# A decayed cumulative sum behind a matmul: new engine orders for the first 40 tiles, and a fourth input buffer

## The chip, the cores and the metric

The kernel runs on one core of a Trainium2 chip. Five engines work side by side, each through its own queue in order: TensorE (PE, the matmuls), VectorE (DVE), ScalarE (ACT), GpSimd (POOL) and SyncE (SP, which here only issues DMAs). The metric is the device time of one execution in microseconds (us); lower is better.

## What is computed

```python
x, w, decay = inputs            # (16, 2048, 1024), (1024, 1024), (1024,), all float32
xw = x @ w                      # per batch: 2048 time steps, 1024 output channels
out[:, 0, :] = xw[:, 0, :]
for t in range(1, S):           # S = 2048
    out[:, t, :] = decay[None, :] * out[:, t - 1, :] + xw[:, t, :]
```

It is a matmul, followed by a running sum over time that shrinks by a factor of its own in every channel.

## The kernel before

**Chunks and tiles.** The time axis of a batch is cut into four chunks of 512 steps, so there are 64 chunks. Two neighbouring chunks make a group. A tile (the code says slot) is one group times one of eight blocks of 128 output channels: 1024 time steps in PSUM, 128 channels on the partitions, and 16 matmuls of 128x512 (eight contraction blocks k, two chunks). Tiles 0 to 7 belong to chunks 0 and 1, tiles 8 to 15 to chunks 2 and 3, and so on. Chunks 0 and 1 hold the first half of a batch, chunks 2 and 3 the second, so tiles 8 to 15 continue the sums of tiles 0 to 7 from saved last columns (keep).

**Input path.** A chunk comes in four loads (L105), each 256 KB in bf16, cast by the DMA and issued from GpSimd's queue into a buffer xb (three of them). VectorE turns it (turn, L115, letter T: 32x32 blocks of two-bf16 words) into xw, and ScalarE sorts it into xt in two parts (part, L123): X for contraction blocks 0 to 3, Y for 4 to 7. At the start chunks 0 and 1 go in smaller pieces: E turns a quarter chunk (half of the time steps, half of the channels), and F (VectorE) or G (ScalarE) copies an eighth. M loads half a chunk.

**Weights.** w comes in eight pieces into the room of output buffers; settle (L299) casts or copies one contraction block for four channel blocks into wsb, as W on VectorE or as w on ScalarE. Pieces 0 to 7 serve tiles 0 to 3, pieces 8 to 15 tiles 4 to 7 (and all later ones): 8 to 11 the even k, 12 to 15 the odd k. U loads such a piece's data. D makes the decay columns and their squares.

**Scans.** An unpaired tile is scanned by VectorE straight from PSUM, 1024 elements long (S, L216). A paired tile is done at half that length: ScalarE copies PSUM to xs (p, L178) and makes decay times the even steps (g, L164), GpSimd adds that to the odd steps (j, L191), VectorE scans the 512 odd steps with the squared decay (S, L196), ScalarE multiplies the result by the decay (h, L164) and GpSimd adds it to the even steps (c, L241). P stands for p, g, z and j together, C for h and c (and k, which saves the last column; z puts the starting value in front of the result). Whether a tile is paired is its place among four (three are, the fourth is not), turned around for the tiles in `flips`. The squares lie in SBUF until deed d (L342) puts a second copy into PSUM, which later scans use.

**Output.** VectorE turns the result back (B, L253) into an output buffer; when four tiles are in it, SyncE issues four stores.

**PSUM.** Tiles use three buffers of 1024 columns in turn, so tile s+3 can begin when tile s has left its buffer: by S for an unpaired tile, by p and g for a paired one. Tile 3 lies in two spare buffers; tiles 4, 5 and 6 follow tiles 0, 1 and 2.

**Order.** Everything is issued in program order, and an engine does its queue strictly in that order. The program goes through the tiles; behind the matmuls of each it performs a list of deeds (L547 to L556), each a letter and a number: S5 is the scan of tile 5, T4 the turn of chunk 4, L the next load in `loads`. Which deeds stand behind which tile is written out by hand in `agenda` for the prologue (-99), the first 17 and the last 20 tiles; between them usual() makes the list, with the turns and copies of chunks at set distances ahead (`later`). A deed's place against other engines' deeds does not matter, only its place in its own engine's queue.

```python
        self.paired = n % R != R - 1
        if len(tiles) in flips or len(tiles) - len(slots) in flips:
            self.paired = not self.paired
```

Of the kernel before, what the change touches and what calls it, by code (L numbers as in the profile page):

```python
# [25 lines left out]
def kernel(  # L26
# [31 lines left out]
    NQ = 4  # L58
# [17 lines left out]
    def ring(pool, name, count, shape, dtype=FP32):  # L76
        i = turns[name] = turns.get(name, -1) + 1
        return pool.tile(shape, dtype, name=f"{name}{i % count}")
# [22 lines left out]
    def load(c, q, j0=0, j1=NJ):  # L101
        b, t0 = chunks[c]
        if c not in xb_of:
            xb_of[c] = ring(sb, "xb", 3, [128, NJ, CQ], BF16)
        pin(nc.gpsimd.dma_start(  # L105
            out=xb_of[c][quad(q), j0:j1],
            in_=_ap(x, [[D, P], [P * D, j1 - j0], [1, CQ]],
                    (b * S + t0 + j0 * P) * D + q * CQ)))
# [246 lines left out]
    def ending(i):  # L355
        b, t0 = chunks[-1]
        nb = TL // 128
        pts = [ring(psp, name, count, [128, R, 128])
               for name, count in (("spare1", 1), ("ps", 3), ("ps", 3), ("spare", 1))]
        wides = [ring(sb, *spot, [128, NQ, R, P])  # L360
                 for spot in (("xb", 3), ("xb", 3), ("xb", 3), ("h", 4))]

        def cross(blocks, rs):
            for i in blocks:
                for r in rs:
                    t = 2 + i * 128
                    pin(nc.tensor.transpose(  # L367
                        out=pts[i][:, r], in_=tiles[r - R].so[:, t:t + 128], identity=ident))

        def leave(i, copy):  # L370
            pin(copy(out=wides[i].rearrange("p q r i -> p r q i"),
                     in_=pts[i].rearrange("p r (q i) -> p r q i", q=NQ)))
            pin(nc.sync.dma_start(
                out=_ap(out, [[D, 128], [1, CH]], (b * S + t0 + i * 128) * D + CH),
                in_=wides[i].rearrange("p q r i -> p (q r i)")))

        cross((0,), range(R))
        cross((1,), range(R))
        cross((2, 3), range(R - 1))
        cross((2, 3), (R - 1,))  # L380
        for i in range(nb):
            leave(i, (nc.scalar.copy, nc.vector.tensor_copy)[i % 2])
# [2 lines left out]
    slots += [([c], n) for c in groups[-1] for n in range(K)]  # L385
    tiles = []

    def turn_and_load(c):
        turn(c)
        if 2 <= c < nch - 3:  # L390
            loads.extend((c + 3, q) for q in range(NQ))

    loads = [(c, q) for c in (2, 3, 4) for q in range(NQ)]
    deeds = {
        "P": lambda s: tiles[s % len(slots)].pair(),
        "S": lambda s: tiles[s % len(slots)].scan(),
        "C": lambda s: tiles[s % len(slots)].complete(),
        "B": lambda s: tiles[s % len(slots)].back(),
        "T": turn_and_load,
        "X": lambda c: part(c, nc.scalar.copy, 0, 2),  # L400
        "Y": lambda c: part(c, nc.scalar.copy, 2, M),
        "x": lambda c: part(c, nc.vector.tensor_copy, 0, 2),
# [21 lines left out]
        "L": lambda i: load(*loads.pop(0)) if loads else None,  # L424
    }
    agenda = {
        -99: "M0 M1 U0 U1 M2 M3 U2 U3 W0 w1 L E0 F0 G1 E1 L F2 D G3 E2 F4 L G5 W2 E3 F6 w3 G7 W4 W6 w5 w7 E4 F8 G9 E5 F10 G11 E6 F12 G13 E7 F14 G15 W8 W10 W9 W11",
        0: "P0 L w15 w13",
        1: "L L L S0 C0",
        2: "L P2 P1 w12 S1 L L B0 B1 S2",  # L430
        3: "w14 C2 T2",
        4: "S3 P4 X2 Y2 T3 C1",
        5: "",
        6: "L L P5 L B3 L L S4 L S5 B2 C3 X3 Y3 C4 T4",
        7: "P6 C5 S7 X4 S6",
        8: "C7 C6 L d P8 B4 B7 B6",
        9: "B5 P9",
        10: "L S8 P10 C8 T5 X5 L S9",
        11: "L L S11 L C9 Y4 S10 C10 B8",
        12: "",  # L440
        13: "B11 P12 B10 B9 Y5 S12 P13 C12",
        14: "L P14 T6 S13 C13 L Y6 L",
        15: "L S15 L S14 C14",
        16: "B13 B12 B15 B14 P16 X6",
        -20: "z-20",
        -19: "p-20 g-20",
        -18: "j-20 S-19 S-20 k-19 B-19",
# [15 lines left out]
        -2: "S-3 S-4",  # L463
        -1: "S-2 h-4 c-4 a-1 b-1 V",
    }
    flips = (0, 1, -19, -18, -16, -11, -8, -6, -3, -2)
    later = {10: ["Y4"]}
    for c in range(5, nch):
        first = c // 2 * K
        ahead = (7, 6, 4) if c % 2 else (11, 10, 8)  # L470
        for letter, a in zip("TXY", ahead):
            later.setdefault(first - a, []).append(f"{letter}{c}")

    def usual(s):
        paired = [t.paired for t in tiles]
# [25 lines left out]
    for step, (g, n) in enumerate(slots):  # L501
        T = TL * len(g)
        left = step - len(slots)
        if n % R == 0:
            ns, nj = range(n, n + R), T // P
            outlets = [Outlet(ns, nj)]
        if left == -R:
            outlets = []
        if step == 0:
            heads = [ring(psp, "ps", 3, [128, T]) for _ in range(3)]  # L510
            firsts = [ps[:, 0:TL] for ps in heads] + [spares[0]]
            seconds = [ps[:, TL:T] for ps in heads] + [spares[1]]
            for j0, j1 in halves:
                for k in (0, 2):
                    for i in range(R):
                        matmul(firsts[i], i, k, xt_of[0], j0 * P, j1 * P)
            for k in (4, 6, 1, 3, 5, 7):
                for i in range(R):
                    matmul(firsts[i], i, k, xt_of[0])
            for k0 in range(0, K, 4):  # L520
                for i in range(R):
                    for k in range(k0, k0 + 4):
                        matmul(seconds[i], i, k, xt_of[1], 0, H * P)
            for i in range(R):
                for k in range(K):
                    matmul(seconds[i], i, k, xt_of[1], H * P, TL, H * P)
        if step < R:
            ps = heads[n] if n < 3 else tuple(spares)
        else:
            if len(g) == 2 or n % R < 3:  # L530
                ps = ring(psp, "ps", 3, [128, T])
            else:
                ps = ring(psp, "spare", 1, [128, TL])
            todo = [(k, l) for k in range(K) for l in range(len(g))]
            if step < K:
                todo.sort(key=lambda kl: kl[0] % 2)
            elif step == K:
                todo.sort(key=lambda kl: kl[1])
            if left == -1:
                ps = tuple(both[:, t:t + TL // 2] for t, both in zip(  # L540
                    (0, TL // 2), (ps, ring(psp, "ps", 3, [128, TL]))))
                for t, half in zip((0, TL // 2), ps):
                    for k in range(K):
                        matmul(half, n, k, xt_of[g[0]], t, t + TL // 2, t)
                todo = []
            for k, l in todo:
                matmul(ps[:, l * TL:(l + 1) * TL], n, k, xt_of[g[l]])  # L547
        tiles.append(Tile(g, n, ps, outlets))
        do = agenda.get(step, agenda.get(left) if left >= -20 else None)
        if do is None:  # L550
            do = usual(step)
        else:
            do = do.split()
            if left == -20:
                do = rest(step) + do
        perform(do)  # L556
# [29 lines left out]
```

## Time and profile before

| | |
|---|---|
| time, median of 5 runs | 910.46 us (910.19 to 912.15) |
| the profiled execution's own time | 909.47 us |
| its span, first to last instruction | 907.4 us |
| TensorE busy | 895.1 us, 99% of the span |
| VectorE, ScalarE, GpSimd busy | 830.0, 679.8, 655.0 us |
| first matmul on data | 10.16 us |
| tile 4, tile 9 begin | 28.48, 47.49 us |
| granted TensorE clock | 1.000 |

The span leaves out what lies around the program's instructions, here 2.1 us. Busy time of TensorE is the union of its matmuls, which overlap each other; how fast it works is better read from how many matmuls fit in a stretch. Rows of the timeline give the start and the length of an instruction, or of several alike that follow each other (xN), and in brackets the idle time of the engine before it with what ended that.

### The profile page before, as it was taken

To read this page: it belongs to the slowest core of one execution; us is meant where nothing else is said; L and a number is where in the kernel's file an instruction comes from. 1 tells how busy PE (TensorE), PEld (TensorE's weight loads), DVE (VectorE), ACT (ScalarE), POOL (GpSimd) and SP (SyncE) were. 2 spreads that over 40 slices of the span, in tenths; PEclk is the share of its full clock that TensorE was granted. 3 is DMA by queue.
4 is the path that set the end of the run, shared out by engine and by line. 5 is a ranking of instruction groups with operands and counts; after the bars stand their busy time and mean duration, and the time that the engine had idled before them with its cause. 6 is when DMAs were issued, how large, how long until landed. Compare 5 with 4: busy or idle time off the path is not lost.

```text
span 907.4 us, 12011 instructions
## 1 busy us (share of the span) xinstructions
PE 895.1 (99%) x4187; PEld 409.9 (45%) x4187; DVE 830.0 (91%) x620; ACT 679.8 (75%) x940; POOL 655.0 (72%) x754
## 2 busy tenths in 40 slices
PE   7999999999999999999999999999999999999997
PEld 3544444444444444444444444444444444444444
DVE  4999999999999999999999999999999999999998
ACT  3787887877777778778778777787787787787742
POOL 7677978777777777677687776777777776876632
PEclk9999999999999999999999999999999999999999
DMA  9999999999999999999999999999999999999868
GB/s 166 175 222 236 216 215 253 245 258 251 243 244 249 242 231 234 221 231 231 223 234 221 231 229 224 236 228 226 233 228 228 224 237 222 227 230 213 178 143 235
DMA packets 402604, 204.48 MB, mean 225 GB/s; under 512 B 8816, under 2 KB 401776, under 8 KB 402544
## 3 DMA queue, kind: packets, MB, share of 16 engines
q1 hardware_dynamic: 265200, 134.76, 59.6%
q0 software_dynamic: 137344, 68.96, 57.0%
q8 instruction: 32, 0.52, 0.2%
q14 instruction: 28, 0.23, 0.1%
HBM read 138.42 MB, written 134.22 MB: 300 GB/s over the span
## 4 chain that ended last, share of the span: by engine, by line
PE 94%; DMA 2%; ACT 1%; DVE 1%; POOL 1%; issue 0%; DVEq 0%; POOLq 0%
PE ps L126 93%; DMA xb<-in_x_dram 1%; ACT xt L123 1%; PE spare L126 1%; DMA ot<-in_w_dram 1%; DVE so L216 0%; POOL ot L291 0%; ACT h L164 0%; POOL xb L105 0%; ACT xs L178 0%; DVE ot L253 0%; DVE so L196 0%; PE spare L367 0%; DVE wsb L299 0%; PE ps L367 0%
## 5 line engine op out<-in xcount | busy, mean ns | idle before, releaser
L126 PE MATMUL ps<-xt,wsb 128*128 128x512 bf16 (+1 forms) x4086 | 877.9, 377 | 5.4 <-DVE xt L123 2.8
L126 PEld LDWEIGHTS <-wsb 128*128 128x128 bf16 x4144 | 405.2, 98 | 485.9 <-issue 5.8
L191 POOL TENSOR_TENSOR xs<-h,xs 128x512 f32<-128x512 f32 (+1 forms) x188 | 240.5, 1279 | 200.8 <-ACT h L164 96.6
L178 ACT COPY xs<-ps 128x1024 f32<-128x1024 f32 (+1 forms) x188 | 187.7, 998 | 156.8 <-PE ps L126 155.0
L253 DVE STREAM_TRANSPOSE ot<-so 128x1024 f32<-128x1024 f32 (+1 forms) x260 | 299.8, 1191 | 0.8
L241 POOL TENSOR_TENSOR so<-h,xs 128x512 f32<-128x512 f32 (+1 forms) x188 | 239.5, 1274 | 38.5 <-ACT h L164 21.7
L123 ACT COPY xt<-xw 128x2048 bf16<-128x2048 bf16 (+1 forms) x132 | 240.6, 1824 | 9.6 <-DVE xw L115 9.6
L105 POOL DMA_DIRECT2D xb<-in_x_dram x264 | 174.0, 660 | 1.6 <-POOLq L570 0.9
L164 ACT ACTIVATE h<-so,dec 128x512 f32<-128x512 f32 (+1 forms) x188 | 144.0, 766 | 30.1 <-DVE so L196 26.7
L115 DVE STREAM_TRANSPOSE xw<-xb 128x2048 f32<-128x2048 f32 (+1 forms) x70 | 147.4, 2106 | 6.4 <-DMA xb<-in_x_dram 6.3
L196 DVE TENSOR_TENSOR_SCAN so<-spare,keep,xs 128x512 f32<-128x512 f32 (+1 forms) x96 | 119.5, 1245 | 28.2 <-POOL xs L191 27.8
L196 DVE TENSOR_TENSOR_SCAN so<-spare,xs 128x512 f32<-128x512 f32 x88 | 107.6, 1222 | 27.6 <-POOL xs L191 24.8
L164 ACT ACTIVATE h<-ps,dec 128x512 f32<-128x512 f32 (+1 forms) x188 | 129.0, 686 | 0.0
L216 DVE TENSOR_TENSOR_SCAN so<-dec,ps 128x1024 f32<-128x1024 f32 x35 | 79.0, 2260 | 0.6 <-ACT h L164 0.6
L216 DVE TENSOR_TENSOR_SCAN so<-dec,keep,ps 128x1024 f32<-128x1024 f32 (+1 forms) x36 | 77.1, 2143 | 0.1
L245 ACT COPY keep<-so 128x1 f32<-128x1 f32 x136 | 25.5, 187 | 12.5 <-DVE so L216 12.5
L187 ACT COPY so<-keep 128x1 f32<-128x1 f32 x96 | 18.3, 191 | 1.9 <-DVE ot L253 1.9
L126 PE MATMUL spare<-xt,wsb 128*128 128x512 bf16 (+1 forms) x58 | 12.3, 328 | 0.0
L185 POOL MEMSET so<- 128x1 f32 x92 | 10.7, 116 | 1.1 <-ACT keep L245 1.1
L291 POOL DMA_DIRECT2D ot<-in_w_dram x16 | 8.7, 541 | 3.3 <-DMA xb<-in_x_dram 1.7
L309 PE MATMUL spare<-idle 128*128 128x512 bf16 x27 | 7.5, 447 | 2.3 <-ACT idle L307 2.3
L299 ACT COPY wsb<-ot 128x512 bf16<-128x512 bf16 x7 | 4.0, 616 | 5.1 <-DMA ot<-in_w_dram 5.1
(32 smaller groups left out, 33.2 us busy)
## 6 DMA issues: line engine op xcount, KB each, us to landing
out_dram<-ot SPq DMA_DIRECT2D x248, 512.0 KB, 10.6
xb<-in_x_dram POOLq DMA_DIRECT2D x248, 256.0 KB, 7.6
out_dram<-ot SPq DMA_DIRECT2D x12, 256.0 KB, 4.4
xb<-in_x_dram POOLq DMA_DIRECT2D x16, 128.0 KB, 5.3
ot<-in_w_dram POOLq DMA_DIRECT2D x12, 128.0 KB, 5.3
out_dram<-xb SPq DMA_DIRECT2D x3, 256.0 KB
ot<-in_w_dram SPq DMA_DIRECT2D x4, 128.0 KB, 3.4
ot<-in_w_dram POOLq DMA_DIRECT2D x4, 64.0 KB, 4.5
```

The costliest lines, as they stand in the source:

```text
L105: pin(nc.gpsimd.dma_start(out=xb_of[c][quad(q), j0:j1], in_=_ap(x, [[D, P], [P * D, j1 - j0], [1, CQ]], (b * S + t0 + j0 * P) * D + q * CQ)))
L115: pin(nc.vector.transpose(out=dst.rearrange("p (m j i) -> p j m i", m=M, i=P)[:, j0:j1, m0:m1], in_=src.rearrange("p (j m c) -> p j m c", ...
L123: pin(copy(out=xt_of[c][:, m0:m1, :, j0 * P:j1 * P], in_=src))
L126: pin(nc.tensor.matmul(out=ps[:, t0:t1] if ps.shape[1] >= t1 else ps, lhsT=wsb[:, k, n].rearrange("p q i -> p (q i)"), rhs=xt[:, k // 2, k ...
L164: pin(nc.scalar.activation(out=h, in_=src, func=mybir.ActivationFunctionType.Copy, scale=dec[:, self.n:self.n + 1]))
L178: pin(nc.scalar.copy(out=self.xs, in_=self.ps))
L191: pin(nc.gpsimd.tensor_tensor(out=odds, in0=self.g, in1=odds, op=ALU.add))
L196: pin(nc.vector.tensor_tensor_scan(out=so[:, 3:T + 2:2], data0=squares[-1][:, n:n + 1].to_broadcast([128, T // 2]), data1=self.xs[:, 1:T:2 ...
L216: pin(nc.vector.tensor_tensor_scan(out=so[:, t + 2:t + 2 + size], data0=dec[:, n:n + 1].to_broadcast([128, size]), data1=ps, initial=befor ...
L241: pin(nc.gpsimd.tensor_tensor(out=self.so[:, 2:T + 2:2], in0=self.h, in1=self.xs[:, 0:T:2], op=ALU.add))
L245: pin(nc.scalar.copy(out=self.keep, in_=self.so[:, self.T + 1:self.T + 2]))
L253: pin(nc.vector.transpose(out=outlet.ot[:, :, c0:c0 + P], in_=self.so[:, 2 + t0:2 + t0 + nj * P].rearrange("p (i t) -> p i t", t=P)))
```

## The change

The orders of the prologue and of the tiles 0 to 41 are written anew, most of them in single steps (p, g, z, j, h, c, k) rather than in P and C, and other tiles among the first 40 are paired: 0, 2, 3, 10, 17, 20, 22, 24, 28, 31, 35, 37, 38 and 39 are unpaired now, where before it was 0, 1 and every fourth from 3 on. Chunk 2 is turned in two halves (t, u), chunk 3 too. Tiles 8 and 9 are computed together: both use chunk 2 first, then chunk 3. The input has four buffers instead of three, so the loads run one chunk further ahead. Turns of chunks 4 to 13 and copies up to chunk 12 are in the lists, so `later` begins with chunk 14 or 13.

```diff
@@ -101,7 +101,7 @@
     def load(c, q, j0=0, j1=NJ):
         b, t0 = chunks[c]
         if c not in xb_of:
-            xb_of[c] = ring(sb, "xb", 3, [128, NJ, CQ], BF16)
+            xb_of[c] = ring(sb, "xb", 4, [128, NJ, CQ], BF16)
         pin(nc.gpsimd.dma_start(
             out=xb_of[c][quad(q), j0:j1],
             in_=_ap(x, [[D, P], [P * D, j1 - j0], [1, CQ]],
@@ -358,7 +358,7 @@
         pts = [ring(psp, name, count, [128, R, 128])
                for name, count in (("spare1", 1), ("ps", 3), ("ps", 3), ("spare", 1))]
         wides = [ring(sb, *spot, [128, NQ, R, P])
-                 for spot in (("xb", 3), ("xb", 3), ("xb", 3), ("h", 4))]
+                 for spot in (("xb", 4), ("xb", 4), ("xb", 4), ("h", 4))]
 
         def cross(blocks, rs):
             for i in blocks:
@@ -385,18 +385,28 @@
     slots += [([c], n) for c in groups[-1] for n in range(K)]
     tiles = []
 
-    def turn_and_load(c):
-        turn(c)
-        if 2 <= c < nch - 3:
-            loads.extend((c + 3, q) for q in range(NQ))
-
-    loads = [(c, q) for c in (2, 3, 4) for q in range(NQ)]
+    def turn_half(half):
+        def act(c):
+            if half == 0:
+                turn(c, 0, NJ, 0, 2)
+            else:
+                turn_and_load(c, 2)
+        return act
+
+    def turn_and_load(c, m0=0):
+        turn(c, 0, NJ, m0, M)
+        if 2 <= c < nch - 4:
+            loads.extend((c + 4, q) for q in range(NQ))
+
+    loads = [(c, q) for c in (2, 3, 4, 5) for q in range(NQ)]
     deeds = {
         "P": lambda s: tiles[s % len(slots)].pair(),
         "S": lambda s: tiles[s % len(slots)].scan(),
         "C": lambda s: tiles[s % len(slots)].complete(),
         "B": lambda s: tiles[s % len(slots)].back(),
         "T": turn_and_load,
+        "t": turn_half(0),
+        "u": turn_half(1),
         "X": lambda c: part(c, nc.scalar.copy, 0, 2),
         "Y": lambda c: part(c, nc.scalar.copy, 2, M),
         "x": lambda c: part(c, nc.vector.tensor_copy, 0, 2),
@@ -424,24 +434,49 @@
         "L": lambda i: load(*loads.pop(0)) if loads else None,
     }
     agenda = {
-        -99: "M0 M1 U0 U1 M2 M3 U2 U3 W0 w1 L E0 F0 G1 E1 L F2 D G3 E2 F4 L G5 W2 E3 F6 w3 G7 W4 W6 w5 w7 E4 F8 G9 E5 F10 G11 E6 F12 G13 E7 F14 G15 W8 W10 W9 W11",
-        0: "P0 L w15 w13",
-        1: "L L L S0 C0",
-        2: "L P2 P1 w12 S1 L L B0 B1 S2",
-        3: "w14 C2 T2",
-        4: "S3 P4 X2 Y2 T3 C1",
-        5: "",
-        6: "L L P5 L B3 L L S4 L S5 B2 C3 X3 Y3 C4 T4",
-        7: "P6 C5 S7 X4 S6",
-        8: "C7 C6 L d P8 B4 B7 B6",
-        9: "B5 P9",
-        10: "L S8 P10 C8 T5 X5 L S9",
-        11: "L L S11 L C9 Y4 S10 C10 B8",
-        12: "",
-        13: "B11 P12 B10 B9 Y5 S12 P13 C12",
-        14: "L P14 T6 S13 C13 L Y6 L",
-        15: "L S15 L S14 C14",
-        16: "B13 B12 B15 B14 P16 X6",
+        -99: "M0 M1 U0 U1 M2 M3 U2 U3 W0 w1 D E1 E0 G3 G2 F0 F1 E3 E2 G6 G7 W3 F5 G4 W2 W6 w4 W5 W7 E5 E4 G10 F11 G8 F9 E6 E7 L G12 F13 L G15 F14",
+        0: "L W11 w10 L W9 W8 L",
+        1: "S0 L",
+        2: "L p1 z1",
+        3: "L w15 W14 g1 B0 k0 L w13 w12 j1 S2",
+        4: "L L S1 k2 p4 B2 L g4 h1",
+        5: "j4 t2 k1 c1 u2 X2 L S3 z4 L",
+        6: "p5 L Y2 L B1 k3 L t3 g5 z5 p6 z6",
+        7: "j5 S4 g6 L X3 B3 j6 u3 h4 L S6 L k4 Y3 c4 S5 k6 p7 z7 B4 h5 T4 h6 c5",
+        8: "",
+        9: "d g7 z8 k5",
+        10: "c6 p8 B5 g8 j7 p9 B6 z9 j8 g9 S7 X4",
+        11: "j9 S8 h7 L S9 Y4 L c7 S10",
+        12: "h8 L p11 L T5 c8 g11 h9 L k7",
+        13: "p12 j11 B10 g12 B8 c9 X5 B7 j12",
+        14: "Y5 B9 L L T6 z11 z12 p13 L z13 z14 g13",
+        15: "S11 X6 j13 S12 L h11 S13 h12 c11 Y6",
+        16: "T7 L c12 p14 B11 L g14 h13 j14",
+        17: "B12 z15 p15 c13 S14 g15 X7 j15 B13",
+        18: "L S15 p16 L g16 z16 S17 h15 j16 Y7 c15",
+        19: "S16 h14 L B17 k17 k16 c14 h16 T8 L p18",
+        20: "c16 p19 B14 g18 L X8 j18 B16 z18 L",
+        21: "B15 Y8 S18 z19 L g19 S20 h18 j19 k18",
+        22: "p21 c18 g21 T9 k20 z21 L j21 B18",
+        23: "L S19 B20 h19 L k19 c19 S22",
+        24: "p23 X9 L T10 Y9",
+        25: "L B22 k22 g23 B19 X10 j23 S21 z23 L",
+        26: "p25 S24 k21 g25 L h21 j25 Y10 S23 c21",
+        27: "B24 k23 h23 L p26 B21 c23 g26 T11 L z25 z26",
+        28: "p27 j26 g27 S25 L j27 S26 h25",
+        29: "c25 B23 h26 c26 B25 z27 S28 z29",
+        30: "p29 g29 S27 j29 B26 h27",
+        31: "c27 p30 S29 z30 g30 B27 h29 j30 B28 c29",
+        32: "X11 S30 S31 Y11",
+        33: "B29 p32 z32 B31 g32 h30 j32 T12 c30",
+        34: "p33 z33 g33 S32 X12 j33 B30 S33",
+        35: "Y12 T13 h33 p34 z34 c33 k33",
+        36: "g34 S35 h32 j34 k32 c32 B33 k35",
+        37: "B32 p36 g36 S34 z36 j36 B35 h34 k34 c34",
+        38: "S36 B34 k36 h36 c36 S37",
+        39: "B36 k37 B37 S38",
+        40: "S39 B38 k38 p40 g40 z40 j40 k39 B39 L L",
+        41: "p41 g41 z41 j41 S40 h40 c40 L L",
         -20: "z-20",
         -19: "p-20 g-20",
         -18: "j-20 S-19 S-20 k-19 B-19",
@@ -463,13 +498,15 @@
         -2: "S-3 S-4",
         -1: "S-2 h-4 c-4 a-1 b-1 V",
     }
-    flips = (0, 1, -19, -18, -16, -11, -8, -6, -3, -2)
-    later = {10: ["Y4"]}
+    flips = (0, 2, 7, 10, 11, 15, 17, 19, 20, 22, 23, 24, 27, 28, 37, 38, -19, -18, -16, -11, -8, -6, -3, -2)
+    later = {}
+    begun = {"T": 14, "X": 13, "Y": 13}
     for c in range(5, nch):
         first = c // 2 * K
         ahead = (7, 6, 4) if c % 2 else (11, 10, 8)
         for letter, a in zip("TXY", ahead):
-            later.setdefault(first - a, []).append(f"{letter}{c}")
+            if c >= begun[letter]:
+                later.setdefault(first - a, []).append(f"{letter}{c}")
 
     def usual(s):
         paired = [t.paired for t in tiles]
@@ -527,7 +564,9 @@
         if step < R:
             ps = heads[n] if n < 3 else tuple(spares)
         else:
-            if len(g) == 2 or n % R < 3:
+            if step == K + 1:
+                ps = nexts
+            elif len(g) == 2 or n % R < 3:
                 ps = ring(psp, "ps", 3, [128, T])
             else:
                 ps = ring(psp, "spare", 1, [128, TL])
@@ -535,7 +574,14 @@
             if step < K:
                 todo.sort(key=lambda kl: kl[0] % 2)
             elif step == K:
-                todo.sort(key=lambda kl: kl[1])
+                todo = []
+                nexts = ring(psp, "ps", 3, [128, T])
+                for l in range(len(g)):
+                    for i, both in enumerate((ps, nexts)):
+                        for k in range(K):
+                            matmul(both[:, l * TL:(l + 1) * TL], n + i, k, xt_of[g[l]])
+            elif step == K + 1:
+                todo = []
             if left == -1:
                 ps = tuple(both[:, t:t + TL // 2] for t, both in zip(
                     (0, TL // 2), (ps, ring(psp, "ps", 3, [128, TL]))))
```

## The prediction

> **What bounds the kernel now.** I read the page first (who is busy), then the chain that ended last, then TensorE's waits, then the timelines of the first 60 us engine by engine. From the page and from the chain (start us, us, what):
>
> ```profile
> PE 895.1 (99%) x4187; PEld 409.9 (45%) x4187; DVE 830.0 (91%) x620; ACT 679.8 (75%) x940; POOL 655.0 (72%) x754
> ```
> ```profile
> 47.49 830.73 PE ps L126 x3848
> ```
>
> TensorE is the bound. One full-width matmul takes 830.73 / 3848 = 0.2159 us, a tile of 16 takes 3.454 us, and after 47.49 us it waits for nobody that the waits view lists. So the change can only win what TensorE loses earlier, and can lose by putting a wait where none is now. Its waits, and the stretches of its timeline that end in the last three:
>
> ```profile
> PE ps L126 <- DVE xt L123: 2.8, 4, 1.8
> PE ps L126 <- ACT h L164: 0.8, 1, 0.8
> PE ps L126 <- DVE so L216: 0.7, 1, 0.7
> PE ps L126 <- ACT wsb L299: 0.7, 1, 0.7
> PE ps L126 <- DVE wsb L299: 0.4, 1, 0.4
> ```
> ```profile
> 28.48 1.89 PE L126 MATMUL ps<-xt,wsb 128*128 128x512 bf16 x8 [0.67 <-DVE so L216]
> 31.02 15.71 PE L126 MATMUL ps<-xt,wsb 128*128 128x512 bf16 x72 [0.66 <-ACT wsb L299]
> 47.49 2.75 PE L126 MATMUL ps<-xt,wsb 128*128 128x512 bf16 x12 [0.76 <-ACT h L164]
> ```
>
> Tile 4 begins at 28.48, waits again at 31.02, and tile 9 waits until 47.49. These waits are 5.4 us together; about 0.1 us of pipeline drain comes on top of each, so some 6.1 us is the most that can be won: 0.7% of the time. In the other direction the head has little slack. The stretch of 42 to 60 us (busy us in the order PE, PEld, DVE, ACT, POOL) and two ones behind it:
>
> ```profile
> 42.00:60.00 18.00, 17.24 (x80) 7.74 (x79) 18.00 (x15) 15.05 (x23) 13.91 (x16) 1.00 1.08 187
> 60.00:80.00 20.00, 20.00 (x94) 9.08 (x93) 18.86 (x14) 16.50 (x20) 16.32 (x18) 1.00 1.25 245
> 80.00:110.00 30.00, 30.00 (x141) 13.58 (x139) 29.27 (x23) 25.90 (x38) 26.44 (x33) 1.00 1.30 220
> ```
>
> VectorE is busy for all of 18.00 us: its queue has a backlog here.
>
> **The change, step by step.** Durations are rows of this trace; on an engine that waits for nothing the next instruction starts about 0.08 us (VectorE) or 0.1 us (ScalarE) before the last ends, so a queue is summed at: turn 2.21, half turn or back 1.14, paired scan 1.11 to 1.17, unpaired scan 2.18 to 2.24, copy p 0.91, g 0.58, h 0.67, X or Y 1.80, weight copy on ScalarE 0.52.
>
> *Prologue.* The loads keep their order, and D is free: VectorE idles 7.11 to 8.93 anyway. Turning E1 before E0 costs a start: chunk 0's first half can be turned at 8.93, two turns (0.63 + 0.71) and F0 end at 10.74, first matmul 10.79 instead of 10.16. The second half lands at 11.52: E3 and E2 end at 12.97, and G4 is now third on ScalarE behind G6 and G7: 12.39 + 2 x 0.52 + 0.62 = 14.05, against 13.00 before. Then 8 half-width (0.108 each) and 8 full matmuls, to 16.69; the k=1 weights moved from VectorE (0.29) to ScalarE (0.62): 17.16, then 16 matmuls to 20.61. Chunk 1 is again turned upper part first and its first quarter copied second on ScalarE: 21.48 against 20.66. Then 64 half-width matmuls (6.94) end at 28.42. The PSUM buffer that tile 4 needs is freed by S0: tile 0 ends at 26.0, S0 takes 2.27: 28.3. So every delay up to here is swallowed by waits that were there: 28.42 against 28.48.
>
> *Tile 4's odd weights.* ScalarE from the end of tile 1: 26.93 + p1 0.91 + w15 0.52 + g1 0.58 + k0 0.08 + w13 0.52 + w12 0.62 = 30.16. TensorE arrives at 30.15 and starts again at 30.2, not 31.02: 0.8 us won. Tiles 5, 6, 7 and 8 begin at 31.93, 35.38, 38.84 and 42.29.
>
> *Tiles 8 and 9.* Sixteen matmuls on chunk 2 come first, so chunk 3 is needed at 45.75 and its upper part (Y3) at 46.61, and tile 6's PSUM already at 44.02. ScalarE: X2 waits for t2 (35.2), then p5, Y2, k3, g5 to 40.5, p6, g6 to 42.0: in time, so today's wait at 47.49 (0.9 us with its drain) goes. What is late next is found on VectorE. Its queue from 26.05: S0, W14 28.25, B0 28.45, S2 29.59, S1 31.77, B2 32.88, t2 34.02, u2 35.16, S3 36.30 (two scans, 2.50), B1 38.80, t3 39.94, S4 41.08, then B3, u3, S6, S5, B4. With no disturbance u3 ends at 44.53, Y3 at 46.5 (0.1 us to spare) and B4 starts at 46.7.
>
> *The disturbance.* Timelines and source rows of a paired scan whose factor (squares) lies in SBUF:
>
> ```profile
> 42.11 2.99 DVE L196 TENSOR_TENSOR_SCAN so<-squares,xs 128x512 f32<-128x512 f32 x2
> L196 DVE TENSOR_TENSOR_SCAN so<-squares,xs x4: 1180/1191/1870, 32.8 to 50.5; 128x512 f32<-128x512 f32 x4
> ```
> ```profile
> 41.61 1.29 POOL L191 TENSOR_TENSOR xs<-h,xs 128x512 f32<-128x512 f32 x1 [1.43 <-ACT keep L245]
> ```
>
> The first scan of the row at 42.11 is the one of these four that met a GpSimd addition, and took 1.87 us instead of 1.19: 42.11 to 43.98, that is 1.08 us after the addition ended at 42.90. The three others met none. The change keeps four such scans (S1, S4, S6, S5 stand ahead of d) and packs the additions closer. The load ahead of j5 waits for a DMA slot that frees when chunk 4's first quarter lands (39.96), so j5 runs 40.85 to 42.15, with S4 at 41.08 inside it: S4 ends at 42.15 + 1.08 = 43.23. Then B3, u3 44.29 to 45.49, Y3 45.54 to 47.44: TensorE waits 0.85 us at 46.61. S6 at 45.43 meets c4 (45.37 to 46.67) and ends at 47.75; S5 at 47.67; B4 at 48.78 instead of 46.7. ScalarE's g7, behind h5 and h6, ends at 51.0, and tile 10 begins at 51.05, against 50.94 before. [...]
>
> *Tiles 10 to 41.* VectorE now has no idle time planned: from B4 to the end of T6 stand 7 backs 7.98, T4 and T5 4.42, S7 1.13, S8 and S9 2.34, S10 2.24, d 0.07, T6 2.29 = 20.47 us. Behind T6, ScalarE does X6 1.80, h11 0.67, h12 0.67, Y6 1.80, p14 0.91, g14 0.69 before tile 17 has its PSUM: tile 17 cannot start before B4 + 27.07. With B4 at 48.78 that is 75.85; before it was 47.49 + 8 x 3.454 = 75.12. So TensorE is 0.7 us later than before. Summed the same way, S24 ends at B4 + 61.0, so tile 27 can start at B4 + 61.06 = 109.84, inside the 0.7 us lag; S28 and S38 leave 1.3 and 0.7 us. Of the first 40 tiles 14 are unpaired, not 12, about 1 us more each for VectorE; that is in these sums.
>
> *Fourth buffer, its loads.* Landings of chunks 2 to 4 are set by the DMA rate (one quarter per 1.34 us, 28.96 to 44.04), not by buffers; the earlier issues (0.65 us each on GpSimd, counted above where they stand ahead of j1, j5, j6 and c4) bring chunk 5 sooner. No turn waits for a load after the head today, so nothing is won; the slowest load among the first stores took 9.0 us from its issue to its landing (45.41 to 54.41), and chunk 5, issued by 40, has until T5 at 60, so nothing is lost either. The stores of tiles 0 to 3 leave SyncE behind B3 at 44.4 instead of 46.3, and nobody on the path waits for them. From tile 42 and at the end the order is as before.
>
> Sum: profiled execution 909.47 + 0.7 = 910.2. The median shown is 0.99 above that execution, so 911.2 us.
>
> **Rivals.**
> 1. *The scans are not held up* (j5 or c4 start elsewhere, or the 1.87 us row is a single accident). B4 at 46.7, tile 17 at 73.77: 1.35 us earlier than before, 909.1. For it: only one row shows the stretch. Against: j5 and S4 start within 0.2 us of each other, and c4 covers S6 or S5 whichever wins.
> 2. *VectorE's queue loses more* and the kernel ends slower. Place: S24 before tile 27. Today VectorE idles 1.14 us in 60 to 80 and 0.73 us in 80 to 110, mostly for GpSimd's joins. If these 1.87 us stay, tile 27 begins at 48.78 + 61.06 + 1.87 = 111.71 against 109.70: 912.5. It decides from 1.7 us of idle on. For it: the queue is summed without a hole. Against: with the backlog the joins are finished 1 us or more before their scans.
> 3. *The granted clock drops in the prologue.* TensorE's hole grows to 11.7 to 14.1. Today the clock stays 1.00 with a hole of 1.8 us and falls only in the last stretch, 906 to 907.4 us (mean 0.69), some 3.8 us after the last matmul. If 3.8 us of work ran at half speed (an estimate from that row), it would cost 1.9 us: 913.1 on top of my sum. [...]
>
> **How the numbers follow.** My forecast has 0.5, rival 1 0.22, rival 2 0.22, rival 3 0.06. A difference under 0.2% (1.82 us) is about what this kernel's measurement cannot tell from no change: 908.64 to 912.28. The forecast's own range is 910.6 (c4 loses to S6, or half the stretch) to 911.9 (the scan first, the addition waits, B4 at 49.2). Rival 1 spans 908.4 to 909.8, for the 0.6 us that a walk of 20 steps can be off: a third of it is beyond 0.2%. So faster 0.10 (with 0.02 for a prologue that starts better than I walk it), same 0.58, slower 0.32 (rivals 2 and 3, and a tail of the forecast). The range takes in rival 1's span and rival 2, and reaches to 913.3: 908.5 to 913.3.
>
> **What would show it.** Right: tile 4 without a wait near 31, one around 46.6 on xt or around 49 to 51 on ACT h; scans with squares up to 1.9 to 2.3 us; VectorE busy from 26 to 110 without a gap; tile 17 released by ACT h. Wrong: no TensorE wait after 30.2 (rival 1), waits on DVE so at tiles 25 to 27 (rival 2), a clock row under 1.00 (rival 3), or a first matmul that is not later than 10.16.

## The result, and the profile after

The changed kernel takes 910.43 us (median of 40 runs, 909.38 to 912.81) against 909.5 us (72 runs) for the kernel before: a ratio of 1.001, with a 95% interval of 1.0006 to 1.0015. It is 0.9 us slower; 0.7 was forecast. (The 910.46 us shown further up for the kernel before were five of these 72 runs.) The profiled execution took 910.95 us with a span of 909.2 and a mean granted clock of 0.999.

Busy time, from the page, and TensorE's waits in the changed kernel (in total, times, longest, us):

```profile
PE 895.5 (98%) x4187; PEld 410.0 (45%) x4187; DVE 832.3 (92%) x623; ACT 675.3 (74%) x933; POOL 651.2 (72%) x748
```

```profile
PE ps L126 <- ACT xt L123: 3.4, 3, 1.9
PE ps L126 <- ACT h L164: 1.4, 2, 0.9
PE ps L126 <- DVE xt L123: 1.2, 1, 1.2
PE ps L126 <- ACT wsb L299: 0.8, 2, 0.5
```

and its timeline from 11 to 77 us, the pieces that begin with a wait, and tile 4, which does not (start, length, bracket: idle before):

```profile
11.37 0.49 PE L126 MATMUL ps<-xt,wsb 128*128 128x256 bf16 x3 [1.17 <-DVE xt L123]
...
14.35 0.49 PE L126 MATMUL ps<-xt,wsb 128*128 128x256 bf16 x3 [1.94 <-ACT xt L123]
...
17.60 0.82 PE L126 MATMUL ps<-xt,wsb 128*128 128x512 bf16 x3 [0.49 <-ACT wsb L299]
...
21.86 1.47 PE L126 MATMUL ps<-xt,wsb 128*128 128x256 bf16 x12 [0.64 <-ACT xt L123]
...
28.84 1.89 PE L126 MATMUL ps<-xt,wsb 128*128 128x512 bf16 x8
31.08 16.58 PE L126 MATMUL ps<-xt,wsb 128*128 128x512 bf16 x76 [0.34 <-ACT wsb L299]
48.52 2.75 PE L126 MATMUL ps<-xt,wsb 128*128 128x512 bf16 x12 [0.86 <-ACT xt L123]
52.17 24.33 PE L126 MATMUL ps<-xt,wsb 128*128 128x512 bf16 x112 [0.91 <-ACT h L164]
77.02 53.25 PE L126 MATMUL ps<-xt,wsb 128*128 128x512 bf16 x246 [0.51 <-ACT h L164]
```

The wait that stood at tile 9 (47.49) is gone. In its place stand three: for Y3 with 12 of the 32 matmuls of tiles 8 and 9 still to do (48.52), for tile 7's PSUM at tile 10 (52.17) and for tile 14's at tile 17 (77.02). Behind 77.02 nothing waits. VectorE's timeline and GpSimd's, where the three waits come from:

```profile
42.24 2.03 DVE L196 TENSOR_TENSOR_SCAN so<-squares,xs 128x512 f32<-128x512 f32 x1
44.20 1.21 DVE L253 STREAM_TRANSPOSE ot<-so 128x1024 f32<-128x1024 f32 x1
45.34 1.20 DVE L115 STREAM_TRANSPOSE xw<-xb 128x1024 f32<-128x1024 f32 x1
46.46 3.56 DVE L196 TENSOR_TENSOR_SCAN so<-squares,xs 128x512 f32<-128x512 f32 x2
49.95 1.21 DVE L253 STREAM_TRANSPOSE ot<-so 128x1024 f32<-128x1024 f32 x1
```
```profile
41.88 1.30 POOL L191 TENSOR_TENSOR xs<-h,xs 128x512 f32<-128x512 f32 x1
...
46.64 2.29 POOL L241 TENSOR_TENSOR so<-h,xs 128x512 f32<-128x512 f32 x1
```

S4 (42.24) began inside the addition j5 (41.88 to 43.18) and took 2.03 us; S6 and S5 together took 3.56 us against 2.3 undisturbed, and the addition c4, which began just behind S6, took 2.29 instead of 1.30. B4, the first instruction behind them, stands at 49.95. The busy time by stage (columns PE, PEld, DVE, ACT, POOL):

```profile
42.00:60.00 18.00, 16.23 (x76) 7.17 (x74) 18.00 (x15) 16.27 (x22) 15.98 (x16) 1.00 1.34 222
60.00:80.00 20.00, 19.49 (x91) 8.75 (x90) 19.95 (x15) 19.32 (x26) 17.28 (x19) 1.00 1.29 209
80.00:110.00 30.00, 30.00 (x140) 13.62 (x139) 30.00 (x21) 24.88 (x32) 22.74 (x30) 1.00 1.30 218
```

From 42 to 110 us VectorE idles 0.05 us in all. If its queue sets when the head ends, shorter scans must move everything behind them; the first experiment tests that.

### The profile page after: what moved, and what is told of

Read it like the earlier page. It is cut to its first block, busy times and chain, and to the rows that moved or that the text cites. A ratio compares the mean times of both kernels' runs of the same rounds, so it can differ in the third digit from the quotient of the medians.

```text
span 909.2 us, 11992 instructions
## 1 busy us (share of the span) xinstructions
PE 895.5 (98%) x4187; PEld 410.0 (45%) x4187; DVE 832.3 (92%) x623; ACT 675.3 (74%) x933; POOL 651.2 (72%) x748
## 4 chain that ended last, share of the span: by engine, by line
PE 92%; DMA 3%; ACT 1%; DVE 1%; POOL 1%; issue 1%; ACTq 0%; DVEq 0%; POOLq 0%
PE ps L126 92%; DMA xb<-in_x_dram 2%; ACT xt L123 1%; DMA ot<-in_w_dram 1%; PE spare L126 1%; POOL ot L291 1%; DVE xw L115 0%; POOL xb L105 0%; ACT h L164 0%; DVE ot L253 0%; ACT xs L178 0%; DVE so L196 0%; PE spare L367 0%; PE ps L367 0%; DVE h L371 0%
## 5 line engine op out<-in xcount | busy, mean ns | idle before, releaser
L191 POOL TENSOR_TENSOR xs<-h,xs 128x512 f32<-128x512 f32 (+1 forms) x186 | 238.1, 1281 | 201.9 <-ACT h L164 92.9
L178 ACT COPY xs<-ps 128x1024 f32<-128x1024 f32 (+1 forms) x186 | 185.7, 999 | 156.3 <-PE ps L126 153.5
L115 DVE STREAM_TRANSPOSE xw<-xb 128x2048 f32<-128x2048 f32 (+2 forms) x72 | 146.9, 2046 | 3.1 <-DMA xb<-in_x_dram 3.1
L196 DVE TENSOR_TENSOR_SCAN so<-spare,xs 128x512 f32<-128x512 f32 x86 | 104.9, 1220 | 25.4 <-POOL xs L191 22.8
L216 DVE TENSOR_TENSOR_SCAN so<-dec,ps 128x1024 f32<-128x1024 f32 x37 | 83.6, 2260 | 1.0 <-ACT h L164 0.6
L196 DVE TENSOR_TENSOR_SCAN so<-squares,xs 128x512 f32<-128x512 f32 x4 | 6.8, 1724 | 0.2 <-POOL xs L191 0.2
```

What stands on the lines that cost most here:

```text
L115: pin(nc.vector.transpose(out=dst.rearrange("p (m j i) -> p j m i", m=M, i=P)[:, j0:j1, m0:m1], in_=src.rearrange("p (j m c) -> p j m c", ...
L178: pin(nc.scalar.copy(out=self.xs, in_=self.ps))
L191: pin(nc.gpsimd.tensor_tensor(out=odds, in0=self.g, in1=odds, op=ALU.add))
L196: pin(nc.vector.tensor_tensor_scan(out=so[:, 3:T + 2:2], data0=squares[-1][:, n:n + 1].to_broadcast([128, T // 2]), data1=self.xs[:, 1:T:2 ...
L216: pin(nc.vector.tensor_tensor_scan(out=so[:, t + 2:t + 2 + size], data0=dec[:, n:n + 1].to_broadcast([128, size]), data1=ps, initial=befor ...
```

## The experiments

Times are medians of 11 runs. The experiments ran on three chips, each beside runs of the kernel before on the same chip, so experiments of different chips are compared by their distance to the kernel before. The ratios on record are not simply those of the two medians. A trace shows one execution; the last column has its time, since some traced executions lie far from the median.

| run | us | before, same chip | ratio, 95% interval | traced execution |
|---|---|---|---|---|
| early squares | 908.2 | 909.45 | 0.9989, 0.998 to 0.9997 | 909.09 |
| before, early squares | 909.23 | 909.45 | 0.9998, 0.9989 to 1.0006 | 909.57 |
| tile 14 first | 911.33 | 909.45 | 1.0025, 1.0016 to 1.0034 | 910.79 |
| early squares and tile 14 first | 908.34 | 909.45 | 0.9989, 0.998 to 0.9997 | 908.94 |
| old prologue | 912.0 | 909.39 | 1.0022, 1.0013 to 1.003 | 910.7 |
| tile 8 alone | 910.15 | 909.39 | 1.0016, 1.0005 to 1.0028 | 909.99 |
| before, four buffers | 909.41 | 909.39 | 0.9995, 0.9986 to 1.0004 | 909.87 |
| early squares, tiles 14 and 7 first | 908.65 | 909.39 | 0.9992, 0.9983 to 1.0001 | 909.43 |
| early squares, old prologue | 908.48 | 909.03 | 0.9992, 0.9983 to 1.0001 | 908.0 |
| early squares, tile 38 first | 907.87 | 909.03 | 0.9984, 0.9975 to 0.9993 | 907.23 |
| early squares, old prologue, tile 38 first | 907.9 | 909.03 | 0.9985, 0.9976 to 0.9994 | 907.78 |
| before, four buffers, loads earlier | 908.7 | 909.03 | 0.9996, 0.9987 to 1.0004 | 908.09 |

**Early squares: the held scans.** The one suspected cause is taken away: the scans S4, S6 and S5 read their factor from PSUM.

```diff
-        5: "j4 t2 k1 c1 u2 X2 L S3 z4 L",
+        5: "j4 t2 k1 c1 u2 X2 L S3 d z4 L",
-        9: "d g7 z8 k5",
+        9: "g7 z8 k5",
```

> The changed kernel with the second copy of the squares (d) made right behind S3 and ahead of S4, so S4, S6 and S5 take their factor from PSUM. Theory A (scans and GpSimd additions hold each other up, and VectorE's queue from B4 on sets when tile 17 may start): the three scans take about 1.2 us each instead of 2.03, 1.40 and 2.23, GpSimd's c4 1.3 instead of 2.29, B4 starts at about 47.9 instead of 49.95, the waits near 48.5 (1.0 us) and 52.2 (1.1) shrink to 0.2 and 0.4, tile 17 begins 2.0 us earlier than 77.02. Time about 908.4, 2.0 us under the changed kernel and 1.1 under the kernel before. Rival B (the order on ScalarE alone makes these waits): no difference to the changed kernel, 910.4 within 0.4. Rival C (the later first matmul shifts everything): the same, 910.4.

908.2 us: 1.25 us under the kernel before on the same chip, where the changed kernel is 0.9 over it. VectorE's and GpSimd's timelines of this run:

```profile
41.46 1.18 DVE L196 TENSOR_TENSOR_SCAN so<-spare,xs 128x512 f32<-128x512 f32 x1
42.57 1.21 DVE L253 STREAM_TRANSPOSE ot<-so 128x1024 f32<-128x1024 f32 x1
43.70 1.20 DVE L115 STREAM_TRANSPOSE xw<-xb 128x1024 f32<-128x1024 f32 x1
44.83 2.30 DVE L196 TENSOR_TENSOR_SCAN so<-spare,xs 128x512 f32<-128x512 f32 x2
47.05 1.20 DVE L253 STREAM_TRANSPOSE ot<-so 128x1024 f32<-128x1024 f32 x1
```
```profile
41.10 1.31 POOL L191 TENSOR_TENSOR xs<-h,xs 128x512 f32<-128x512 f32 x1
...
45.59 1.30 POOL L241 TENSOR_TENSOR so<-h,xs 128x512 f32<-128x512 f32 x1
```

S4 still meets j5, and the pair S6 and S5 still meets c4, but no scan and no addition is stretched. From the start of S4 to B4 pass 5.59 us (47.05 - 41.46) instead of 7.71. TensorE's waits shrink as expected, and a new one appears far behind:

```profile
46.88 2.75 PE L126 MATMUL ps<-xt,wsb 128*128 128x512 bf16 x12 [0.26 <-ACT xt L123]
49.90 107.43 PE L126 MATMUL ps<-xt,wsb 128*128 128x512 bf16 x486 [0.26 <-ACT h L164]
158.15 12.03 PE L126 MATMUL ps<-xt,wsb 128*128 128x512 bf16 x54 [0.82 <-DVE so L216]
```

Rivals B and C, by which nothing should have changed, fall. By its medians the edit is worth 2.2 us, 2.0 were expected.

**The same edit in the kernel before.**

```diff
-        4: "S3 P4 X2 Y2 T3 C1",
+        4: "S3 d P4 X2 Y2 T3 C1",
-        8: "C7 C6 L d P8 B4 B7 B6",
+        8: "C7 C6 L P8 B4 B7 B6",
```

> The kernel before with d right behind S3. Theory A: the scan at 42.11 takes 1.2 us instead of 1.87, but in that kernel nothing on TensorE's path hangs on it, since ScalarE's copies ahead of tile 9 are ordered ahead of what waits for the scan; the wait at 47.49 stays 0.9 us and the time does not change (within 0.3 us). If a long scan always costs TensorE its excess: 0.7 us faster.

No difference that can be measured, as expected, though the trace does not show it in the way expected: the wait at tile 9 did not stay, it shrank from 0.76 to 0.30 us, and a new one of 0.73 us stands at tile 22. In this execution VectorE was ahead and then waited for a load (1.30 us ahead of T7, where the kernel before waited 0.52), as its timeline and TensorE's show (the last runs come back to that):

```profile
84.94 2.31 DVE L115 STREAM_TRANSPOSE xw<-xb 128x2048 f32<-128x2048 f32 x1 [1.30 <-DMA xb<-in_x_dram]
```
```profile
92.84 77.43 PE L126 MATMUL ps<-xt,wsb 128*128 128x512 bf16 x351 [0.73 <-DVE so L216]
```

**Tile 14's PSUM first.** Alone, and with the early squares.

```diff
-        15: "S11 X6 j13 S12 L h11 S13 h12 c11 Y6",
-        16: "T7 L c12 p14 B11 L g14 h13 j14",
+        15: "S11 X6 j13 S12 L h11 S13 h12 c11",
+        16: "T7 L c12 p14 B11 L g14 Y6 h13 j14",
```

> The changed kernel with Y6 behind p14 and g14 on ScalarE. Theory A: tile 17's wait of 0.68 us goes, and S24 ahead of tile 27 takes 0.1 to 0.2 of it back (B4 at 49.95 plus 61.06 is 111.0, TensorE would be there at 110.9). Time 0.4 to 0.7 us under the changed kernel: 909.7 to 910.0. Rival B: the whole 0.68 us, no wait at tile 27. Rival C: nothing.

> Both edits. Theory A: tile 17 is released by whichever is later, and once the scans are short TensorE itself arrives at about 74.9, so the second edit adds only 0.1 us to the first: about 908.3, 2.1 us under the changed kernel. Rival B: only the second edit counts, 909.7 to 909.9. Rival C: 910.4.

The first is a miss: 911.33, slower than the changed kernel instead of 0.4 to 0.7 us faster. Tile 17's wait went, but ScalarE's timeline shows why nothing was won by it:

```profile
73.58 1.01 ACT L178 COPY xs<-ps 128x1024 f32<-128x1024 f32 x1 [0.76 <-POOL so L241]
74.49 0.69 ACT L164 ACTIVATE h<-ps,dec 128x512 f32<-128x512 f32 x1
75.07 1.90 ACT L123 COPY xt<-xw 128x2048 bf16<-128x2048 bf16 x1
76.86 0.78 ACT L164 ACTIVATE h<-so,dec 128x512 f32<-128x512 f32 x1
```

p14 writes one of three xs buffers, and tile 11 still reads it in its addition c11. So ScalarE stands idle for 0.76 us, where Y6 had filled the gap, and everything behind is late: TensorE waits at 79.27 for tile 15's PSUM and at 93.92 for tile 19's. The trace shows that the won wait was lost again, and not where the 0.9 us between the two medians come from: in this execution, of 910.79 us, tile 22 begins at 93.92, in the changed kernel's trace at 94.29 (77.02 and five tiles). The long scans (up to 2.58 us in this run) and a lowered clock (below, at rival 3) are candidates that no run here tells apart. With the early squares the second edit adds nothing: 908.34 against 908.2, where 0.1 us of gain was expected. Its wait stands at tile 22:

```profile
92.02 2.96 PE L126 MATMUL ps<-xt,wsb 128*128 128x512 bf16 x13 [0.31 <-ACT h L164]
```

**The old prologue.** Order of turns, copies and weights as before, in the changed kernel.

```diff
-        -99: "... W0 w1 D E1 E0 G3 G2 F0 F1 E3 E2 G6 G7 W3 F5 G4 W2 W6 w4 W5 W7 E5 E4 G10 F11 G8 F9 E6 E7 L G12 F13 L G15 F14",
+        -99: "... W0 w1 E0 F0 G1 E1 F2 D G3 E2 F4 G5 W2 E3 F6 w3 G7 W4 W6 w5 w7 E4 F8 G9 E5 F10 G11 E6 F12 G13 L E7 F14 L G15",
```

> The changed kernel with the old prologue's order of turns, copies and weights on VectorE and ScalarE (D behind F2 again; W8 to W11 stay in tile 0's list). Theory A: the first matmul comes at 10.2 instead of 11.37, but tile 4 begins only 0.2 to 0.4 us earlier (28.4 to 28.6 instead of 28.84), because S0, behind the weights that land at 24.9, ends near 28.3; what is won there moves B4 and tile 17 by the same: 0.2 to 0.4 us faster than the changed kernel, 910.0 to 910.2. Rival C (the later first matmul shifts everything): 1.2 us faster, 909.2.

A miss, and the most telling one. In the traced execution the first matmul came at 10.01 and tile 4 at 26.97, 1.9 us ahead of the changed kernel, and yet the median is 912.0, 1.6 us slower. VectorE and GpSimd:

```profile
40.16 4.28 DVE L196 TENSOR_TENSOR_SCAN so<-squares,xs 128x512 f32<-128x512 f32 x1
```
```profile
40.15 1.30 POOL L191 TENSOR_TENSOR xs<-h,xs 128x512 f32<-128x512 f32 x1
41.38 0.67 POOL L105 DMA_DIRECT2D xb<-in_x_dram  x1
42.06 1.30 POOL L191 TENSOR_TENSOR xs<-h,xs 128x512 f32<-128x512 f32 x1
```

S4 and j5 started within 0.01 us of each other, and S4 was held until j6, the next addition, had ended at 43.36 as well; then it ran its 1.08 us. By its timeline TensorE waited for Y3:

```profile
48.69 2.75 PE L126 MATMUL ps<-xt,wsb 128*128 128x512 bf16 x12 [2.61 <-ACT xt L123]
```

So the held scan used up most of the lead: tile 17 begins at 76.43, 0.6 us ahead of the changed kernel's 77.02, and this execution took 910.7 us, less than the changed kernel's traced 910.95. It is not an execution that lost 1.6 us. What sets the others apart on record is the mean granted clock: six of the 11 have 0.998 and a median of 912.16, the five with 0.999 or 1.0 (the traced one is among them) have 910.98. None of the six was traced.

To tell this from a fault of the old order itself, both edits were made together:

> The changed kernel with the early squares and the old prologue order. With the old prologue alone the scan S4 was held for 4.28 us, through two additions, and TensorE waited 2.6 us for Y3. Theory A (the held scan is why the old prologue lost time): with the squares in PSUM S4 takes 1.2 us, tile 4 begins 0.3 to 0.7 us earlier than with the early squares alone and S38 ahead of tile 41 moves along: 907.5 to 907.9. Rival (the old order itself costs the time): 1.6 us slower than the early squares alone, 909.8.

908.48: the 1.6 us are gone, so the old order itself does not cost them; they come with scans that read their factor from SBUF. How much of them is the holding and how much the lowered clock, which none of the 11 executions shows now, is not told apart. The 0.3 to 0.7 us that the earlier start should bring on top are not there (a difference of 0.3 us either way is not resolved). The order of the prologue is worth nothing that can be measured once the scans are free.

**Tile 8 alone.** The joint order of tiles 8 and 9 undone.

```diff
-            if step == K + 1:
-                ps = nexts
-            elif len(g) == 2 or n % R < 3:
+            if len(g) == 2 or n % R < 3:
...
             elif step == K:
-                todo = []
-                nexts = ring(psp, "ps", 3, [128, T])
-                for l in range(len(g)):
-                    for i, both in enumerate((ps, nexts)):
-                        for k in range(K):
-                            matmul(both[:, l * TL:(l + 1) * TL], n + i, k, xt_of[g[l]])
-            elif step == K + 1:
-                todo = []
+                todo.sort(key=lambda kl: kl[1])
```

> The changed kernel with tile 8 computed alone as before (chunk 2, then chunk 3), then tile 9. Theory A: Y3 at 48.5 is now waited for with four matmuls of tile 8 and all of tile 9 still to do; the wait near 48.5 grows from 1.0 to about 2.8 us but starts earlier, tile 10 begins at 52.8 instead of 52.17, and tile 17, which waits for VectorE's and ScalarE's queues and not for TensorE, still begins near 77.0: 0 to 0.2 us slower than the changed kernel. If the joint order is worth its wait: 0.7 us or more slower, 911.1.

910.15, the changed kernel's time within what is resolved. TensorE loses 2.69 us at one place and then runs on; tile 17 begins at 76.32, 0.05 us behind the end of g14:

```profile
47.71 32.66 PE L126 MATMUL ps<-xt,wsb 128*128 128x512 bf16 x150 [2.69 <-ACT xt L123]
```

So what the joint order wins at tile 10 is taken back at tile 17. That holds for the seven executions with a mean clock of 0.999 (median 909.99, the traced one among them). The other four have 0.994 to 0.997 and took 911.6 to 914.8 us; whether the hole of 2.69 us lowered their clock is not seen, as none of them was traced.

**The fourth buffer, in the kernel before.** First the buffer and the loads of one chunk more, with the orders as they were:

```diff
-            xb_of[c] = ring(sb, "xb", 3, [128, NJ, CQ], BF16)
+            xb_of[c] = ring(sb, "xb", 4, [128, NJ, CQ], BF16)
-                 for spot in (("xb", 3), ("xb", 3), ("xb", 3), ("h", 4))]
+                 for spot in (("xb", 4), ("xb", 4), ("xb", 4), ("h", 4))]
-        if 2 <= c < nch - 3:
-            loads.extend((c + 3, q) for q in range(NQ))
+        if 2 <= c < nch - 4:
+            loads.extend((c + 4, q) for q in range(NQ))
-    loads = [(c, q) for c in (2, 3, 4) for q in range(NQ)]
+    loads = [(c, q) for c in (2, 3, 4, 5) for q in range(NQ)]
```

> The kernel before with four input buffers and loads one chunk further ahead, its orders unchanged. Theory A: no turn waits for a load behind the prologue, so nothing changes: within 0.3 us of the kernel before. Rival: more loads in GpSimd's queue ahead of its additions delay them by 0.65 us each, 0.5 to 1 us slower.

No change, as expected, but not for the reason expected: turns do wait for loads behind the prologue. The buffer could not help, since the lists issue the loads no earlier: in this run as in the kernel before, T7 waits for its chunk.

```profile
85.25 2.31 DVE L115 STREAM_TRANSPOSE xw<-xb 128x2048 f32<-128x2048 f32 x1 [1.39 <-DMA xb<-in_x_dram]
```
```profile
71.19 2.31 DVE L115 STREAM_TRANSPOSE xw<-xb 128x2048 f32<-128x2048 f32 x1 [1.12 <-DMA xb<-in_x_dram]
...
84.22 2.31 DVE L115 STREAM_TRANSPOSE xw<-xb 128x2048 f32<-128x2048 f32 x1 [0.52 <-DMA xb<-in_x_dram]
```

(The second fence is the kernel before.) Then with four of these loads moved up as well:

```diff
-        7: "P6 C5 S7 X4 S6",
+        7: "P6 C5 S7 X4 S6 L L L L",
```

> The kernel before with four input buffers and four more loads in the list of tile 7, where GpSimd idles from 50.1 to 52.6. In that kernel T6 starts at 71.19 and T7 at 84.22, each when its chunk lands (71.06, 84.10), and tile 22 starts 8.0 to 8.3 us behind the landing of chunk 7 in three profiles. Theory D (in the kernel before, the loads hold VectorE's queue and so tile 22): chunks 6 and 7 land 10 us earlier, T6 and T7 no longer wait, tile 22 is no longer held; 0.3 to 0.9 us faster, 908.5 to 909.1. Rival (the landings are beside the path): no change, 909.4.

In its profile no turn waits behind the head and tile 22 begins at 91.14 without a wait. The time, 908.7 against 909.03, is on the expected side, but its interval includes no change: that the loads held the kernel before is seen in the traces (this one is of an execution of 908.09 us, the shortest of its 11), and not settled by the times.

**What is late next.** On top of the early squares: g7 ahead of h5 and h6 (with tile 14 first); and, on the early squares without that, S38 ahead of two backs.

```diff
-        7: "j5 S4 g6 L X3 B3 j6 u3 h4 L S6 L k4 Y3 c4 S5 k6 p7 z7 B4 h5 T4 h6 c5",
+        7: "j5 S4 g6 L X3 B3 j6 u3 h4 L S6 L k4 Y3 c4 S5 k6 p7 g7 z7 B4 h5 T4 h6 c5",
-        9: "g7 z8 k5",
+        9: "z8 k5",
...
-        39: "B36 k37 B37 S38",
+        39: "S38 B36 k37 B37",
```

> Both edits of the squares and of tile 14, and g7 moved ahead of h5 and h6 on ScalarE. Theory A: tile 10 no longer waits for tile 7's PSUM (0.4 us left of the 1.07), tile 17 is free before TensorE arrives, and the next bound, S24 ahead of tile 27, stands at B4 + 61.06, equal to TensorE's own arrival: 0.4 to 0.6 us under the kernel with both edits, about 907.8, 1.7 us under the kernel before. If c5, which now waits 0.6 us longer for h5, holds up B5 on VectorE, tile 27 waits by as much and the gain is 0 to 0.2 us.

> The changed kernel with the early squares, and S38 ahead of B36 and B37 on VectorE. Theory A (VectorE's queue is the bound up to tile 42): the wait of 0.8 to 1.0 us that the early squares left at tile 41 (158.15, on S38) goes; S39 ahead of tile 42 takes back 0 to 0.3 us. Time 907.2 to 907.6, 0.6 to 1.0 us under the early squares alone. Rival (that wait belongs to one profiled execution): no difference, 908.2.

> Early squares, old prologue order and S38 first. Theory A: the two gains lie in different places and add, as far as S39 ahead of tile 42 allows: 906.9 to 907.4, 2.0 to 2.5 us under the kernel before. Rival: no better than the better of the two.

Moving g7 took tile 10's wait away and won nothing (908.65, where about 907.8 was expected): 0.35 us came back at tile 18 and 0.56 at tile 22, both on ScalarE's h. Moving S38 gave the lowest median, 907.87, 0.3 us under the early squares alone, half of what was expected. That gain is not shown: against the kernel before on the same chip it is 1.16 us, for the early squares alone 1.25. The trace has no wait behind 49.12,

```profile
49.12 121.24 PE L126 MATMUL ps<-xt,wsb 128*128 128x512 bf16 x549 [0.16 <-ACT h L164]
```

but neither has that of the early squares with the old prologue, where S38 stands as before and nothing waits behind 49.59, and with tile 14 first nothing waits behind 92.02. So the rival, that the wait at tile 41 belongs to one profiled execution, stands. What is shown is that the changed kernel with early squares, in all its versions, lies 0.55 to 1.25 us under the kernel before by the medians; which of them is best is not resolved. The old prologue adds nothing to S38 first (907.9).

## Why the prediction was right, point by point

**Prologue.** "D is free" was wrong. D began at 8.89 and the first matmul came at 11.37, not 10.79, because, in the waits of the changed kernel,

```profile
DVE cols L333 <- DMA rows<-in_decay_dram: 1.4, 1, 1.4
```

VectorE waited for the decay's rows; in the kernel before D stood so late that this was not to be seen. The waits that follow came where they were put, on ScalarE's copies and on the k=1 weights (14.35, 17.60, 21.86 against 14.10, 17.16, 21.48), each 0.25 to 0.44 us later because the second half of chunk 0, the weights and the chunk behind them landed 0.25 to 0.45 us later in this execution. Tile 4 began at 28.84, not 28.42: of the 1.2 us that the first matmul came later, all but 0.4 was swallowed. In the six other traces with this prologue tile 4 begins at 27.53 to 28.66, so the forecast holds and this execution is a late one.

**Tile 4's odd weights.** Forecast 30.2, measured 31.08: of the 0.8 us nothing was left in this execution. The last piece of weights landed at 28.60, against 27.63 in the execution of before from which the walk took it. Where it landed at 27.57 (early squares) the wait was 0.1 us, and none of the six other traces with this prologue lists a wait there. The mechanism holds; the size hangs on a landing.

**Held scans.** Right in kind and size. S4 was to end at 1.08 us behind the addition and ended 1.09 behind it. S6 was to be held by c4; it came 0.18 us ahead of it, took 1.40 us itself, and c4 was stretched and S5 held instead. From S4 to B4 the walk had 7.70 us, the trace has 7.71: the same sum by another order, which is luck in part (the range of the forecast put B4 0.4 us later for the case of the scan first). The addition c4, which began 0.18 us behind S6, took 2.29 us and ended 1.07 behind S6; with the old prologue a scan was held through two additions with a load issued in between (4.28 us). How the two engines come to hold each other is not shown here.

**Tiles 9 to 17.** The wait for Y3 was forecast at 0.85 us, measured 1.02 with its drain; tile 10's on g7 1.0, measured 1.07. Tile 17 was to begin 27.07 us behind B4: 49.95 + 27.07 = 77.02, and it began at 77.02. With tile 8 alone the same sum comes out again (B4 at 49.25, tile 17 at 76.32); with the old prologue tile 17 is 0.5 us later than by it (48.85, 76.43). B4 itself was 1.2 us later than walked, all of it ahead of S4: late landings, and 0.5 us between the two halves of S3. This second part is no accident: it stands in all seven traces with the new prologue and in none of the three with the old one in the changed kernel. What makes it is not explained. S24 was to stay inside the lag, and tile 27 waited for nothing.

**The fourth buffer.** "No turn waits for a load after the head today" was wrong, though it cost the sum nothing. The waits view has five waits of turns on loads, 6.3 us in all, and two of them, 1.12 and 0.52 us, are T6 and T7 at 71 and 84. The changed kernel has neither of the two. That is a gain which the forecast put at zero by this sentence, and had in its sum all the same, because VectorE's queue was summed without a hole. The same two waits, 1.64 us, are most of the 1.87 us of idle time that rival 2 put down to GpSimd's joins.

**The sum and the rivals.** 0.7 us of lag were forecast, the medians differ by 0.9. The time named, 911.2, was 0.8 too high for another reason: its last term, 0.99 us between the profiled execution and the median, came from five runs, and over 72 runs the median is 909.5, the same as the profiled 909.47. Without that term the walk gives 910.2. That the lag came so near is luck in part: in the two traces tile 17 begins 1.9 us later than before (77.02 against 75.12), 1.2 more than walked, and the spans differ by 1.8. Of that 0.5 is the luck of the execution (910.95 against a median of 910.43), and 0.3 is made up outside the span (1.8 us after, 2.1 before). Rival 1 (scans not held) fell with the early squares, which also show what it would have been: 1.25 us under the kernel before, where 1.35 was given. Rival 2 fell: VectorE had 0.05 us of idle time where 1.7 would have decided.

Rival 3 (the granted clock drops in the prologue) did not show in the profiled execution, with a hole of 1.94 us and a clock of 1.00 from 5 to 110 us, but it did in two of the later traces with this prologue. TensorE's timeline with tile 14 first:

```profile
13.72 0.80 PE L126 MATMUL ps<-xt,wsb 128*128 128x256 bf16 x3 [2.12 <-ACT xt L123]
...
15.38 1.49 PE L126 MATMUL ps<-xt,wsb 128*128 128x512 bf16 x3
...
17.78 0.81 PE L126 MATMUL ps<-xt,wsb 128*128 128x512 bf16 x3
```

Behind the hole TensorE ran at half its pace, three matmuls of 128x512 in 1.49 us in place of 0.81, and at 17.78 at its full one again; the mean granted clock of this execution is 0.997. With tiles 14 and 7 first (mean 0.997 too) it was the same behind a hole of 2.00 us: three took 1.49 us at 14.84 and at 16.55, and 0.81 at 18.22. Behind a hole of 2.20 us (tile 8 alone) three took 0.81 us. So the length of the hole does not tell, in these traces, whether it costs something. Half the pace for 3.4 us (14.84 to 18.22) costs 1.7 us, and half the clock for as long takes 0.002 off the mean of an execution (1.7 of 909 us). On record 24 of the 40 executions of the changed kernel have a mean of 0.996 to 0.998; the 100 of the kernel before that ran beside the experiments all have 0.999 or 1.0. So rival 3 came true in most executions, as far as their mean clock tells. It cost little, where 1.9 us were priced: the 24 have a median of 910.49, the 16 others 910.35, which is still 0.85 us over the kernel before. The early squares have it in five of 11 executions and are 1.25 us ahead all the same.

## What to carry to other kernels

When an engine's queue has a backlog, its sum decides, and a wait removed on the bound engine is only moved to the next place where that queue is due: here at tile 17 (0.51 us), 18 (0.35), 22 (0.31 to 0.56) or 41 (0.82). Walk the backlogged queue to the place where it runs dry before pricing any wait ahead of it. Here a scan with two SBUF inputs and a GpSimd addition that started close together cost one of the two up to 1.4 us, once 3.1, and where they meet shifts with the landing of a load; taking one operand from PSUM removed it (S4, met by the addition, took 1.18 us). And one trace is one execution: set its time and its clock beside those of all runs before a loss is read from it.

## What was not expected of the hardware

With the old prologue a scan held by one addition stayed held through the next one too, 4.28 us in place of 1.19, although GpSimd spent 0.6 us between the two issuing a DMA. In the changed kernel the scan held by j5 went on as soon as j5 ended. What tells the two cases apart is not settled; in the first, scan and addition had started at the same time within 0.01 us.

Holes of 2.00 and 2.12 us between matmuls were followed by matmuls at half the pace (three of 128x512 in 1.49 us in place of 0.81), behind the hole of 2.00 us for some 3.4 us; holes of 1.94 to 2.69 us in other traces were not (0.81 us behind 1.94 and 2.20, 12 in 2.75 us behind 2.61 as in the kernel before at 47.49, 150 in 32.66 us behind 2.69). What decides is not known.

The decay's rows, four DMAs of 1 KB, were issued by 3.95 us and held VectorE until 8.89: they were in place about 5 us after they had been issued, among loads of 128 KB that took 5.9 us in the median of the first 12 us.
